# Q's rotary rows computed once per layer for all heads, lists of best tokens sorted by 32, experts' rows on VectorE, and unread products on TensorE ahead of the experts

## The chip, the cores and the metric

The kernel runs on one core of one Trainium2 chip. What counts is the device time of one execution, in microseconds (us); the profile is of one such execution. PE is TensorE, DVE is VectorE, ACT is ScalarE, POOL is GpSimd, SP is SyncE, which here only issues DMA.

## The reference

Two layers over 1024 tokens of 1024 features, batch 1. In each, the normed input goes through one wide projection, three token mixers (attention, pooling, short convolution) are merged by sigmoid gates, one output projection is added back; then each of 16 experts picks the 128 tokens with the highest routing probability for it and works on them.

```python
q = (rmsnorm(cq, q_norm_g) @ w_uq).reshape(B, S, H, DQK)          # 8 heads, 64 + 32 columns
q_rope = apply_rope(q[..., QK_NOPE:], cos[:, :, None], sin[:, :, None])
kv = (rmsnorm(ckv, kv_norm_g) @ w_ukv).reshape(B, S, H, QK_NOPE + V_HEAD)
...
s = jnp.einsum('bqhd,bkhd->bhqk', q_blk, k).astype(jnp.float32)
p = jax.nn.softmax(s, axis=-1).astype(v.dtype)
...
aff = jax.nn.softmax(jnp.einsum('bsd,de->bse', h, w_router), axis=-1)
top_val, top_idx = lax.top_k(aff.transpose(0, 2, 1), cap)          # cap = 128 tokens per expert
xg = jax.vmap(lambda hb, ib: hb[ib])(h, top_idx)
```

## The kernel before

A product of two fp32 matrices is made of three in the type fp32r: each operand is split into a rounded part `hi` (an ACT cast) and the rest `lo` (a DVE subtraction), and `mm3` (L318) issues hi·hi, lo·hi and hi·lo. `split` (L112) is the pair of cast and subtraction. PSUM tiles of 512 columns come from `ps1`, of 1024 from `ps2`.

A layer runs in stages; the times are those of layer 0 in the trace. The projections end around 500 us. The **gate loop** (500 to 622 with the low-rank parts) makes 8 gate blocks, each a projection of 1024 columns on PE and a sigmoid on ACT that is stored to DRAM. The **attention** (622 to 901) goes over 64 units (head h, query block t). For a unit `scores` (L839) makes 12 products of 512 columns into a `ps2` tile, two units ahead; DVE takes the row maximum, ACT the exponential, both share the division; PE transposes the result (`trans`), and every second unit `av` (L868) multiplies with V. K of two heads is made by `k_pair` (L806), Q of one head by `q_head` (L826): 128 output columns, of which 64 are plain and 64 are the rotary ones in two orders, multiplied by a table of cosines and sines (`tab_e`, `tab_o`) and added inside the score product. The weight of a pair is split in seven pieces to get that order. `rope_part` copies the rotated key into K's tiles.

The **merge** (901 to 950) multiplies the attention output by `w_oa`, 16 blocks (half hf, block d) of 12 products each (`merge_mm`, `merge_gate`); two of them run before the last `av`. The **out-projection loop** (950 to 1062, L1235 to L1262) goes over 8 tiles of 128 tokens: two halves of 24 products (`out_mm`), the residual on DVE, four transposes (`x_trans`), and four router products (`router`) per half, the softmax `soft` into `aff`, and the normed row `h2_rows` by ACT and two POOL operations into DRAM. The best tokens of each expert are found alongside on DVE: tiles are collected in `LISTS`, 16 rounds of maxima each, except tiles 6 and 7, which PE transposes so that 4 rounds over 32 columns do (`quick_sort`, `quick_rounds`, `quick_gather`) and then a merging sort (`quick_list`, `quick_merged`). After each residual `fills(FILL)` issues some of this work.

```python
            t = 7
            x_trans(t, 1)
            scale(t)
            router(t, 1)
            quick_gather(6)
            fills(1000)
            ready = soft(t)
            quick_sort(t)
            quick_rounds(t)
            quick_gather(t)
```

What follows (the **tail**, 1062 to 1096) is one chain: the last lists, the least chosen value, masks `mk`, slots `slot_of`, the 0/1 matrix `both` of an expert (L1379), its products with the values `tv` (`chosen`), the indirect load of rows `xg`, their transposes. Then the **experts** run to 1675. Layer 1 does the same up to 3320.

The kernel is written in program order for each engine, with a scheduler's list that puts independent DVE work between steps; `behind(x)` keeps an instruction after x.

Of the kernel before, what the change touches and what calls it, by code (L numbers as in the profile page):

```python
# [42 lines left out]
FILL = 4  # L43
LISTS = ((0, 2), (2, 2), (4, 1), (5, 1))
# [10 lines left out]
def encoder(ctx, tc, x, c, positions, w_mod, b_mod, norm1_g, w_in, b_gate, q_norm_g, w_uq, kv_norm_g,  # L55
# [79 lines left out]
    tabd = dram.tile([2, 128, S], F32, name="tabd")  # L135
# [12 lines left out]
    for q in range(4):  # L148
        for r in range(4):
            DVE.tensor_copy(krsel[32 * r:32 * r + 32, 32 * q:32 * q + 32], ident[0:32, 0:32])  # L150
# [112 lines left out]
    def rope_tables(ip):  # L263
# [29 lines left out]
        one = ip.tile([128, S], F32, name="one", tag="ra")  # L293
        ACT.activation(sn, sn, AF.Copy, scale=sgn)
        DVE.memset(one, 1.0)
        for (i, r, src) in ((0, 0, one), (0, 64, cs), (0, 96, sn), (1, 0, cs), (1, 32, sn), (1, 64, one)):
            n = 64 if src is one else 32
            SP.dma_start(tabd[i, r:r + n, :], src[r:r + n, :])
# [28 lines left out]
    for l in range(DEPTH):  # L327
# [327 lines left out]
        tab_e = Cq.tile([128, S], F32, name="tab_e")  # L655
        SP.dma_start(tab_e, tabd[0])
        tab_o = Cq.tile([128, S], F32, name="tab_o")
        SP.dma_start(tab_o, tabd[1])
        kwhi = Cq.tile([128, 2, 512], F32R, name="kwhi")
        kwlo = Cq.tile([128, 2, 512], F32R, name="kwlo")  # L660
        with pool("cqt", side="left") as cp:
            def low(w, c0):
                p = ps2()
                proj(p, w, c0)
                return p
# [47 lines left out]
            DVE.tensor_mul(kt_[0:64], p[0:64], tab_o[0:64])  # L713
            DVE.tensor_mul(kt_[64:128], p[64:128], tab_e[64:128])
# [12 lines left out]
            split(kwhi, kwlo, raw.rearrange("p k h c -> p k (h c)"))  # L727
            def prepare(pp):
# [24 lines left out]
            for dp in range(4):  # L753
                wg = block()
                for d in (2 * dp, 2 * dp + 1):
# [14 lines left out]
                    POOL.dma_start(gate0d[l][d], g)  # L770
                    if d == 1:
# [6 lines left out]
        with pool("att", side="right") as ap:  # L778
            vt = ap.tile([128, 8, 8, 128], F32R, name="vt")
            khi = [ap.tile([128, S], F32R, name=f"khi{i}") for i in range(4)]  # L780
            klo = [ap.tile([128, S], F32R, name=f"klo{i}") for i in range(4)]
# [24 lines left out]
            def k_pair(hp):  # L806

                raw = ap.tile([128, 3, 192], F32, name="uq", bufs=1)
                SP.dma_start(raw, w_uq[l][:, 192 * hp:192 * hp + 192].rearrange("(k p) f -> p k f", p=128))
                qw[hp] = [ap.tile([128, 3, 256], F32R, name=f"qw{i}", bufs=1) for i in range(2)]  # L810
# [9 lines left out]
                for (d0, s0, n) in ((0, 0, 96), (96, 80, 16), (112, 64, 16),  # L820
                                    (128, 160, 32), (160, 176, 16), (176, 160, 16), (192, 96, 64)):
                    split(qw[hp][0][:, :, d0:d0 + n], qw[hp][1][:, :, d0:d0 + n], raw[:, :, s0:s0 + n])

            def q_head(h):
                w = qw[h // 2]
                i = h % 2  # L826
                cc = slice(128 * i, 128 * i + 128)
                tab = tab_e if i == 0 else tab_o
                qs[h] = W.tile([128, 2, S], F32R, name="raw", tag="raw", bufs=2)
                for q in range(2):  # L830
                    s_ = slice(512 * q, 512 * q + 512)
                    p = ps1()
                    for k in range(3):
                        mm3(p, w[0][:, k, cc], w[1][:, k, cc], cqhi[:, k, s_], cqlo[:, k, s_], k == 0, k == 2)
                    qf = ap.tile([128, 512], F32, name="pexp", tag="pexp", bufs=3)
                    DVE.tensor_mul(qf, p, tab[:, s_])
                    split(qs[h][:, 0, s_], qs[h][:, 1, s_], qf)

            def scores(h, t):  # L839
# [11 lines left out]
                ACT.activation(e, p, AF.Exp, bias=nm, scale=SCALE, accum_out=sm)  # L851
# [52 lines left out]
            last_o = []  # L904
            units = [(h, t) for h in range(H) for t in range(8)]
            es, phl, po = {}, {}, {}
            for t in range(2):
                v_tile(t)
            k_pair(0)
            q_head(0)  # L910
# [4 lines left out]
            for i in range(1, 4):  # L915
                rope_part(i)
            for n, (h, t) in enumerate(units):
                if n + LA < len(units):
# [18 lines left out]
                if h % 2 == 0 and t == 2:  # L937
                    q_head(h + 1)
# [10 lines left out]
                if h % 2 == 1 and h + 1 < H:  # L949
                    if t == 1:  # L950
                        k_pair(h // 2 + 1)
                    if t == 4:
                        q_head(h + 1)
# [13 lines left out]
            pm = [ps2() for _ in range(2)][1]  # L967
            for d in range(2):
                merge_mm(pm[:, 512 * d:512 * d + 512], wo0, 128 * d, 0)
            av(7, 3, *phl.pop((7, 3)), po[7])  # L970
        psum_open(0, 8)
# [34 lines left out]
        split(wo2[0], wo2[1], wo2_raw)  # L1006
        for d in range(2):
            merge_gate(pm[:, 512 * d:512 * d + 512], 0, d)
        for i, (hf, d) in enumerate(merges):
            if i < 2:  # L1010
                continue
            p = ps1()
            wo, c0 = ((wo0, 0), (wo1, 256), (wo2, 512), (wo2, 512))[d // 2]
            merge_mm(p, wo, 128 * d - c0, hf)
# [38 lines left out]
        with pool("wout", side="left") as op_:  # L1053
# [46 lines left out]
            def quick_sort(t):  # L1100

                pt = ps1()
                for g in range(4):
                    PE.matmul(pt[32 * g:32 * g + 32, 0:32], aff[:, t - 1:t + 1, :], (negid if g in (0, 3) else ident)[:, 32 * g:32 * g + 32],
# [459 lines left out]
```

## Time and profile before

| | before |
|---|---|
| time, median of 3 runs | 3343.34 us (3342.88 to 3346.71) |
| the profiled execution: its time, its span | 3343.92 us, 3342.1 us |
| mean granted PE clock | 0.979 |
| PE busy | 3178.8 us (95%) |
| DVE, ACT, POOL busy | 2434.5 (73%), 1857.3 (56%), 346.5 (10%) |
| DMA | 685.90 MB, 205 GB/s over the span |

A granted clock of 1.00 is 2.4 GHz, 0.50 is 1.2 GHz. In a row of instruction groups, `out<-in` are the program's tile names, `[4.92 <-DVE op L884]` is idle time of the engine before the instruction and what ended it.

### The profile page before, as it was taken

How to read it: one execution, taken by the hardware profiler on the slowest of the kernel's cores; microseconds unless marked ns; L12 is line 12 of the kernel's file. 1: busy time of each engine (PE TensorE's matmuls, PEld its weight loads, DVE VectorE, ACT ScalarE, POOL GpSimd, SP SyncE). 2: the span in 40 equal slices, each digit the busy share in tenths (PEclk: the TensorE clock that was granted, in tenths of full speed). 3: DMA queues.
4: the chain of work that ended last, by engine and by line, in shares of the span. 5: the costliest groups of instructions: out<-in, count | busy, mean ns of one | idle time of the engine just before them, and what ended most of it. 6: DMA issues, size and time to landing. Idle time of an engine off the chain costs nothing.

```text
span 3342.1 us, 41527 instructions
## 1 busy us (share of the span) xinstructions
PE 3178.8 (95%) x15825; PEld 2616.3 (78%) x15825; DVE 2434.5 (73%) x3738; ACT 1857.3 (56%) x2535; POOL 346.5 (10%) x356
## 2 busy tenths in 40 slices
PE   6999999999997999999989999999999969999996
PEld 5888887788786788888778888887887858888875
DVE  5555525499868899999854445347998589999997
ACT  5111213488744888887631122226886448888876
POOL 2001011000023001010020000010000331001010
PEclk8999999999998999999999999999999979999998
DMA  6346334100366899999622354340005659999995
GB/s 225 120 138 205 130 125 137 64 18 7 117 221 233 314 394 380 389 389 373 245 60 82 128 165 139 104 164 24 14 28 164 227 211 366 390 390 380 387 381 182
DMA packets 279271, 685.90 MB, mean 205 GB/s; under 512 B 24934, under 2 KB 131648, under 8 KB 279072
## 3 DMA queue, kind: packets, MB, share of 16 engines
q1 hardware_dynamic: 242912, 563.13, 45.5%
q0 software_dynamic: 33856, 111.74, 10.6%
q10 hardware_dynamic: 2304, 8.39, 0.7%
q8 instruction: 124, 2.03, 0.2%
q14 instruction: 75, 0.61, 0.1%
HBM read 607.63 MB, written 75.55 MB: 204 GB/s over the span
## 4 chain that ended last, share of the span: by engine, by line
PE 79%; DVE 12%; ACT 4%; issue 2%; DMA 2%; POOL 1%; SPq 0%; POOLq 0%; DVEq 0%; ACTq 0%
PE ps L325 63%; PE pa L325 4%; PE pa L1149 4%; DVE wlo L115 4%; DVE mx L846 2%; PE pa L864 2%; PE ps L1353 1%; PE pa L872 1%; PE pa L874 1%; ACT whi L115 1%; ACT pexp L851 1%; PE pa L1189 1%; DVE af L1072 1%; DVE pexp L854 1%; DVE T L115 0%
## 5 line engine op out<-in xcount | busy, mean ns | idle before, releaser
L115 DVE TENSOR_TENSOR wlo<-rg,whi 128x1024 fp32r<-128x1024 f32 x768 | 899.6, 1220 | 97.9 <-ACT whi L115 95.1
L115 ACT CAST whi<-rg 128x1024 fp32r<-128x1024 f32 x768 | 763.8, 1048 | 180.1 <-PE ps L325 180.0
L325 PE MATMUL ps<-whi,T 128*128 128x512 f32 x3072 | 841.5, 393 | 3.6 <-ACT T L115 2.2
L325 PEld LDWEIGHTS ps<-whi,T 128*128 128x128 f32 x3072 | 574.4, 189 | 125.6 <-ACT T L115 3.1
L325 PE MATMUL ps<-wlo,T 128*128 128x512 f32 x1536 | 488.1, 399 | 5.0 <-DVE wlo L115 2.6
L325 PE MATMUL ps<-hhi,whi 128*128 128x512 f32 x1376 | 427.3, 392 | 0.0
L325 PE MATMUL ps<-hlo,whi 128*128 128x512 f32 x1376 | 424.0, 389 | 0.0
L325 PE MATMUL ps<-hhi,wlo 128*128 128x512 f32 x1376 | 423.7, 389 | 0.0
L115 ACT CAST whi<-raw 128x2048 fp32r<-128x2048 f32 (+2 forms) x63 | 108.7, 1726 | 428.0 <-PE ps L325 370.5
L325 PEld LDWEIGHTS ps<-wlo,T 128*128 128x128 f32 x1536 | 281.0, 189 | 74.3 <-DVE wlo L115 18.6
L325 PEld LDWEIGHTS ps<-hhi,whi 128*128 128x128 f32 x1376 | 256.9, 188 | 58.8 <-issue 4.2
L325 PEld LDWEIGHTS ps<-hlo,whi 128*128 128x128 f32 x1376 | 258.3, 188 | 54.2
L325 PEld LDWEIGHTS ps<-hhi,wlo 128*128 128x128 f32 x1376 | 258.3, 188 | 54.1
L115 DVE TENSOR_TENSOR wlo<-raw,whi 128x2048 fp32r<-128x2048 f32 (+2 forms) x63 | 130.1, 2065 | 99.9 <-ACT whi L115 99.8
L325 PE MATMUL ps<-khi,raw 128*128 128x512 f32 x512 | 165.8, 405 | 7.2 <-ACT pexp L851 5.7
L115 DVE TENSOR_TENSOR wlo<-pa,whi 128x512 fp32r<-128x512 f32 x256 | 169.5, 681 | 1.1 <-ACT whi L115 0.9
L851 ACT ACTIVATE pexp<-ps,nm 128x1024 f32<-128x1024 f32 x128 | 143.2, 1119 | 30.3 <-DVE nm L848 27.8
L846 DVE TENSOR_REDUCE mx<-ps 128x1 f32<-128x1024 f32 x128 | 155.0, 1213 | 4.3 <-PE ps L325 3.5
L1446 POOL DMA_INDIRECT xres<-y,idx x30 | 72.5, 2416 | 779.4 <-DVE y L1445 779.4
L115 ACT CAST whi<-pa 128x512 fp32r<-128x512 f32 x256 | 139.6, 588 | 6.2 <-PE pa L864 5.0
L229 DVE SCALAR_TENSOR_TENSOR macc<-raw,csil,macc 128x256 f32<-128x256 f32 x280 | 135.0, 484 | 8.4
L864 PE MATMUL pa<-ident,pexp 128*128 128x128 f32 x1024 | 135.2, 273 | 2.6 <-DVE nm L848 1.8
(412 smaller groups left out, 4626.9 us busy)
## 6 DMA issues: line engine op xcount, KB each, us to landing
rg<-in_w_gate_dram SPq DMA_DIRECT2D x128, 1024.0 KB, 8.9
rg<-in_w_up_dram SPq DMA_DIRECT2D x128, 1024.0 KB, 7.0
rg<-in_w_down_dram SPq DMA_DIRECT2D x128, 1024.0 KB, 7.8
raw<-in_w_mod_dram SPq DMA_DIRECT2D x48, 1024.0 KB, 5.3
raw<-in_w_in_dram SPq DMA_DIRECT2D x43, 1024.0 KB, 5.2
part<-pr POOLq DMA_DIRECT2D x32, 512.0 KB, 3.9
pr<-part POOLq DMA_DIRECT2D x16, 512.0 KB, 4.4
sq<-in_w_out_dram POOLq DMA_DIRECT2D x16, 512.0 KB, 4.7
```

Of the source, the lines that this page charges most:

```text
L115: return ACT.copy(hi, src), DVE.tensor_sub(lo, src, f(hi))
L229: DVE.scalar_tensor_tensor(acc, raw[:, k], csil[:, k:k + 1], acc, op0=OP.mult, op1=OP.add)
L325: PE.matmul(dst[:, s], a, b[:, s], start=start and i == 0, stop=stop and i == 2)
L846: DVE.reduce_max(mx, p, axis=AX.X)
L851: ACT.activation(e, p, AF.Exp, bias=nm, scale=SCALE, accum_out=sm)
L854: DVE.tensor_scalar(e[:, :NORM_DVE], e[:, :NORM_DVE], ri, None, op0=OP.mult)
L864: PE.transpose(p[:, 128 * k:128 * k + 128], e[:, o:o + 128], ident)
L872: PE.matmul(po[:, o:o + 256], vt[:, k, h, :], phi[:, k, :], start=(k == 0), stop=False, skip_group_check=True)
L874: PE.matmul(po[0:64, o:o + 256], vt[:, k, h, 0:64], plo[:, k, :], start=False, stop=(k == 7), skip_group_check=True)
L1072: DVE.match_replace(a, v[:, 15 - r, :], a, -1.0)
L1149: PE.matmul(p[c_], a, b, start=(k == 0 and i == 0), stop=(k == 7 and i == 2))
L1446: POOL.indirect_dma_start(out=xres[l], in_=y, in_offset=None, compute_op=OP.add, out_offset=bass.IndirectOffsetOnAxis(ap=idx[e][:, 0:1], a ...
```

## The change

- **Q.** `q_rope` computes the 8 x 32 rotary rows of Q of all heads in one go in gate block 3 (two blocks of 128 rows), rotates them with tables of cosine and sine, splits them and stores them to `qrd` in DRAM. `q_pair` makes the 64 plain columns of two heads at once, and loads the rotary rows of each from `qrd`, held behind the fourth-last exponential. `q_head`, the weight in two orders and the second table go.
- **The attention's start.** K and Q of the first pair come ahead of the V tiles, their weights are loaded in gate block 4, and the rotated key is copied to K's other tiles in units 2, 9 and 17.
- **The merge.** Four blocks instead of two are made before the attention's PSUM tiles are given back, two of them behind the last `av`; the third weight slice is split behind the last sum.
- **The lists.** Tiles 4 to 7 are sorted by 32, `FILL` is 6; `aff_trans` comes one step later. The first half of list 6 is sorted ahead of tile 7's softmax.
- **Rows.** From tile 3 (`OWN`) DVE makes the normed rows in place of ACT and POOL.
- **Unread products.** `keep_on` issues n fp32 products of 128 x 128 into a PSUM tile that nobody reads: 9, 10, 28, 7, 5 and 15 at six places of the tail.
- `both` of expert 0 is made in two halves.

```diff
+    def keep_on(tile_, by, n):
+        with behind(by):
+            for _ in range(n):
+                PE.matmul(tile_, ident, ones, start=True, stop=True, skip_group_check=True)
...
+            def q_rope(raw):
+                w = [W.tile([128, 3, 2, 8, 16], F32R, name=n_, tag=n_) for n_ in ("whi", "wlo")]
...
+                for i in range(2):
+                    p = ps2()
+                    for k in range(3):
+                        mm3(p, w[0][:, k, i], w[1][:, k, i], cqhi[:, k], cqlo[:, k], k == 0, k == 2)
+                    ps.append(p)
...
+                for i, (a, b) in enumerate(((cos, sin), (sin, cos))):
+                    DVE.tensor_mul(r[2 * i], ps[0], a)
+                    DVE.tensor_mul(r[1], ps[1], b)
+                    (DVE.tensor_add if i else DVE.tensor_sub)(r[2 * i], r[2 * i], r[1])
+                    lo = r[2 * i].bitcast(F32R)
+                    split(hi, lo, r[2 * i])
+                    for part, src in enumerate((f(hi), r[2 * i])):
+                        POOL.dma_start(qrd[l][:, 16 * i:16 * i + 16, part, :], src)
...
+            def q_pair(hp):
...
+                    for o in (0, 32):
+                        ld = SP.dma_start(f(qs[h][r + o:r + o + 32]), qrd[l][h])
+                        if last_exp:
+                            gated(ld, last_exp[-4])
...
-                        mm3(p, w[0][:, k, cc], w[1][:, k, cc], cqhi[:, k, s_], cqlo[:, k, s_], k == 0, k == 2)
-                    qf = ap.tile([128, 512], F32, name="pexp", tag="pexp", bufs=3)
-                    DVE.tensor_mul(qf, p, tab[:, s_])
-                    split(qs[h][:, 0, s_], qs[h][:, 1, s_], qf)
+                        mm3(p, w[0][:, k], w[1][:, k], cqhi[:, k, s_], cqlo[:, k, s_], k == 0, k == 2)
+                    for i in range(2):
+                        r = slice(64 * i, 64 * i + 64)
+                        split(qs[2 * hp + i][r, 0, s_], qs[2 * hp + i][r, 1, s_], p[r])
...
             av(7, 3, *phl.pop((7, 3)), po[7])
+            for d in range(2, 4):
+                merge_mm(pms[d], wo1, 128 * d - 256, 0)
...
-        split(wo2[0], wo2[1], wo2_raw)
+        with behind(*last_o[-1]):
+            split(wo2[0], wo2[1], wo2_raw)
...
-                POOL.tensor_mul(xn, xn, a2)
-                POOL.tensor_add(xn, xn, sh2)
+                if t >= OWN:
+                    DVE.scalar_tensor_tensor(xn, xo, rss[t], a2, op0=OP.mult, op1=OP.mult)
+                    DVE.tensor_add(xn, xn, sh2)
...
             def aff_trans(t):
-                if t == 6:
+                if t > 3:
                     quick_sort(t)
                     quick_rounds(t)
                     return
...
-                out_mm(t, p, 1, 4, 7)
-                router(t, 0)
+                out_mm(t, p, 1, 5, 7)
+                if t > 0:
+                    router(t, 0)
+                if t > 4:
+                    quick_gather(t - 1)
                 out_mm(t, p, 1, 7, 8)
...
-            router(t, 1)
-            quick_gather(6)
+            stored = h2_rows(t)
+            idle = ps1()[:, 0:128]
+            keep_on(idle, router(t, 1), 9)
             fills(1000)
+            quick_half(6)
             ready = soft(t)
-            quick_sort(t)
+            keep_on(idle, quick_sort(t), 10)
             quick_rounds(t)
-            quick_gather(t)
+            keep_on(idle, quick_gather(t), 28)
+            with behind(ready):
+                quick_merged(6)
```

On PE, at the end of the loop and in the tail, before (the last out-projection products are L1149, transposes of the residual L1175, gathers of the maxima L1121, router L1189, sort transposes L1104, least value L1298):

```order
2809 L1149 MATMUL pa<-whi,rg 128x512
2810 L1175 MATMUL pa<-ident,xo 128x128 x4
2811 L1121 MATMUL pa<-topl,negid 16x32
2812 L1121 MATMUL pa<-topl,ident 16x32
...
2815 L1189 MATMUL pa<-wra,hT 128x16 x4
2816 L1104 MATMUL pa<-negid,aff 32x32
2817 L1104 MATMUL pa<-ident,aff 32x32 x2
2818 L1104 MATMUL pa<-negid,aff 32x32
...
2822 L1121 MATMUL pa<-topl,ident 16x32
2823 L1298 MATMUL pa<-ident,least 128x16
```

and now (L1216, L1246, L1181, L1260, L1163, L1389 in the same roles):

```order
2762 L1216 MATMUL pa<-whi,rg 128x512
2763 L1181 MATMUL pa<-topl,negid 16x32
2764 L1181 MATMUL pa<-topl,ident 16x32
...
2767 L1246 MATMUL pa<-ident,xo 128x128 x4
2768 L1260 MATMUL pa<-wra,hT 128x16 x4
2769 L130 MATMUL pa<-ones,ident 128x128 x9
2770 L1163 MATMUL pa<-negid,aff 32x32
...
2772 L1163 MATMUL pa<-negid,aff 32x32
2773 L130 MATMUL pa<-ones,ident 128x128 x10
...
2777 L1181 MATMUL pa<-topl,ident 16x32
2778 L130 MATMUL pa<-ones,ident 128x128 x28
2779 L1389 MATMUL pa<-ident,least 128x16
```

The gather of tile 6 moved from behind the residual's transposes to ahead of the last residual, and the unread products (L130) stand between the steps of the chain.

On DVE, at the merge, before (`gh` is a merge gate, `op` the sum of the last head pair, `olo` its rest, `wlo<-raw` of 2048 columns the third weight slice):

```order
750 L986 TENSOR_TENSOR gh<-ps,gh 128x512 x2
751 L987 TENSOR_TENSOR gh<-gh 128x512 x2
752 L115 TENSOR_TENSOR wlo<-raw,whi 128x2048
753 L884 TENSOR_TENSOR op<-pa,otmp 64x512
754 L115 TENSOR_TENSOR olo<-op,ohi 128x512
755 L115 TENSOR_TENSOR rg<-gh,rg 128x512 x2
```

and now:

```order
707 L1045 TENSOR_TENSOR gh<-ps,gh 128x512 x2
708 L1046 TENSOR_TENSOR gh<-gh 128x512 x2
709 L941 TENSOR_TENSOR op<-pa,otmp 64x512
710 L117 TENSOR_TENSOR olo<-op,ohi 128x512
711 L117 TENSOR_TENSOR wlo<-raw,whi 128x2048
712 L117 TENSOR_TENSOR rg<-gh,rg 128x512 x2
```

The sum and its split now stand ahead of the weight slice.

## Rows read from the trace of the kernel before

**Rows 1.** Windows: us, busy us per engine (instructions), PE clock, DMA share, GB/s.

```profile
560.00:620.00 60.00, 60.00 (x268) 49.69 (x267) 13.39 (x15) 8.35 (x7) 10.13 (x19) 1.00 0.52 174
620.00:640.00 20.00, 16.56 (x71) 12.77 (x70) 12.35 (x21) 11.27 (x21) 0.53 (x1) 1.00 0.17 57
640.00:660.00 20.00, 18.17 (x100) 15.23 (x99) 16.86 (x34) 16.40 (x28) 0.00 (x0) 1.00 0.00 0
670.00:860.00 190.00, 188.63 (x1195) 164.56 (x1194) 176.72 (x353) 159.62 (x292) 1.60 (x3) 1.00 0.06 21
904.00:910.30 6.30, 4.03 (x10) 3.16 (x11) 4.17 (x5) 1.66 (x3) 0.00 (x0) 0.50 0.57 206
1020.00:1060.00 40.00, 37.67 (x202) 30.87 (x201) 38.28 (x176) 20.10 (x38) 16.55 (x10) 1.00 0.42 160
1064.40:1068.00 3.60, 2.11 (x16) 1.99 (x16) 1.29 (x9) 2.72 (x5) 0.00 (x0) 0.50 1.01 413
```

**Rows 2.** PE's waits, 900 to 1062: line, releaser, us in total, times, longest.

```profile
PE pa L325 <- DVE op L884: 4.9, 1, 4.9
PE pa L1221 <- DVE aff L1201: 2.4, 3, 0.8
...
PE pa L1104 <- DVE aff L1201: 0.8, 1, 0.8
```

**Rows 3.** Timeline of PE, tail: start us, us, instruction, [idle before <-releaser].

```profile
1064.46 1.89 PE L1189 MATMUL pa<-wra,hT 128*128 128x16 f32 x8 [0.40 <-DVE hT L1178]
...
1074.68 0.29 PE L1121 MATMUL pa<-topl,negid 128*16 128x32 f32 x2 [6.57 <-DVE topl L1113]
...
1084.06 0.25 PE L1298 MATMUL pa<-ident,least 16*128 16x16 f32 x1 [8.77 <-DVE least L1296]
...
1094.65 1.97 PE L1364 MATMUL pa<-ident,xg 128*128 128x128 f32 x8 [4.00 <-DMA xg<-h2d,idx]
1096.44 1.22 PE L325 MATMUL ps<-whi,T 128*128 128x512 f32 x2
...
1098.30 1.09 PE L325 MATMUL ps<-whi,T 128*128 128x512 f32 x4
```

**Rows 4.** Timeline of PE at the merge.

```profile
906.27 0.80 PE L325 MATMUL pa<-ohi,whi 128*128 128x512 f32 x1 [4.92 <-DVE op L884]
...
909.85 0.63 PE L325 MATMUL pa<-ohi,wlo 128*128 128x512 f32 x1
...
911.34 0.39 PE L325 MATMUL pa<-olo,whi 128*128 128x512 f32 x1
...
913.85 0.39 PE L325 MATMUL pa<-ohi,whi 128*128 128x512 f32 x1
```

**Rows 5.** Instruction groups, 620 to 902: count, busy us, mean ns, idle before.

```profile
L325 PE MATMUL pa<-cqhi,qw 128*128 128x512 f32 x96 | 31.1, 392 | 1.4 <-ACT qw L115 1.4
...
L115 DVE TENSOR_TENSOR klo<-pa,khi 64x512 fp32r<-64x512 f32 x16 | 10.6, 683 | 1.8 <-ACT khi L115 1.7
```

**Rows 6.** DMA issues, 620 to 900: count, KB each, median us to landing.

```profile
gh<-gate SPq DMA_DIRECT2D x3, 256.0 KB, 3.2
```

**Rows 7.** Timeline of ACT and of DVE at the merge.

```profile
901.28 1.90 ACT L115 CAST whi<-raw 128x2048 fp32r<-128x2048 f32 x1 [4.36 <-PE pa L872]
...
903.21 2.29 DVE L115 TENSOR_TENSOR wlo<-raw,whi 128x2048 fp32r<-128x2048 f32 x1 [1.19 <-ACT whi L115]
```

**Rows 8.** Timeline of DVE and of POOL in the tail.

```profile
1068.29 0.20 DVE L1089 TENSOR_TENSOR ll<-ll 16x64 f32<-16x64 f32 x1
...
1068.53 2.27 DVE L1090 TENSOR_TENSOR ll<-ll 16x64 f32<-16x64 f32 x1
...
1071.28 2.27 DVE L1090 TENSOR_TENSOR ll<-ll 16x64 f32<-16x64 f32 x1
...
1068.38 2.34 POOL L1211 TENSOR_TENSOR xn<-xn,a 128x1024 f32<-128x1024 f32 x1 [4.64 <-ACT xn L1210]
```

**Rows 9.** Timeline of PE in the low-rank part (fp32 products L685).

```profile
510.23 1.88 PE L685 MATMUL ps<-sq,ones 128*128 128x512 f32 x4
...
512.41 0.63 PE L325 MATMUL ps<-hlo,whi 128*128 128x512 f32 x2
```

More of the change, by code (lines that the diff above doesn't have):

```diff
@@ L134, in encoder @@
     gate0d = [dram.tile([8, 128, S], F32, name=f"gate0{l}") for l in range(DEPTH)]
-    tabd = dram.tile([2, 128, S], F32, name="tabd")
+    tabd = dram.tile([3, 128, S], F32, name="tabd")
+    qrd = [dram.tile([8, 32, 2, S], F32, name=f"qrd{l}") for l in range(DEPTH)]
     woutd = [dram.tile([8, 128, D], F32, name=f"woutd{l}") for l in range(DEPTH)]
@@ L147, in encoder @@
     krsel = consts.tile([128, 128], F32, name="krsel")
-    for q in range(4):
+    DVE.memset(krsel, 0.0)
+    for q in (0, 2):
         for r in range(4):
@@ L292, in rope_tables @@
         DVE.tensor_scalar(sgn, sgn, 0.125, -1.0, op0=OP.mult, op1=OP.add)
[L293 to L298, printed above, removed]
+        turned = ip.tile([128, S], F32, name="turned", tag="ra")
+        ACT.activation(turned, sn, AF.Copy, scale=sgn)
+        SP.dma_start(tabd[0], cs)
+        SP.dma_start(tabd[1], sn)
+        for (r, src) in ((0, cs), (32, turned), (64, cs), (96, turned)):
+            SP.dma_start(tabd[2, r:r + 32, :], src[r:r + 32, :])
     def rms_scale(src, n, scr):
@@ L806, in k_pair @@
             def k_pair(hp):
-                raw = ap.tile([128, 3, 192], F32, name="uq", bufs=1)
-                SP.dma_start(raw, w_uq[l][:, 192 * hp:192 * hp + 192].rearrange("(k p) f -> p k f", p=128))
-                qw[hp] = [ap.tile([128, 3, 256], F32R, name=f"qw{i}", bufs=1) for i in range(2)]
+                raw = uq0 if hp == 0 else uq_load(hp)
+                qw[hp] = [ap.tile([128, 3, 2, 64], F32R, name=f"qw{i}", bufs=1) for i in range(2)]
+                split(qw[hp][0], qw[hp][1], raw.rearrange("p k (i c) -> p k i c", c=96)[:, :, :, 0:64])
                 cc = slice(128 * hp, 128 * hp + 128)
@@ L914, in encoder @@
                 v_tile(t)
-            for i in range(1, 4):
-                rope_part(i)
             for n, (h, t) in enumerate(units):
+                if n in (2, 9, 17):
+                    with behind(last_exp[-1]):
+                        rope_part((2, 9, 17).index(n) + 1)
                 if n + LA < len(units):
@@ L1154, in residual @@
                 added = DVE.tensor_add(xo[:, s_], xo[:, s_], p[hf])
+                if t == 7:
+                    if hf == 0:
+                        gained[t] = op_.tile([128, D], F32, name="xn", tag="xo", bufs=3)
+                    DVE.tensor_mul(gained[t][:, s_], xo[:, s_], a2[:, s_])
                 scr = op_.tile([128, 512], F32, name="hT", tag="hT", bufs=3)
@@ L1207, in h2_rows @@
                 POOL.dma_start(xres[l][sl, :], xo)
-                xn = op_.tile([128, D], F32, name="xn", tag="xo" if t == 7 else "xn", bufs=3 if t == 7 else 1)
-                with behind(softs[-1]):
-                    ACT.activation(xn, xo, AF.Copy, scale=rss.pop(t))
-                POOL.tensor_mul(xn, xn, a2)
-                POOL.tensor_add(xn, xn, sh2)
+                if t == 7:
+                    xn = gained.pop(t)
+                    DVE.scalar_tensor_tensor(xn, xn, rss[t], sh2, op0=OP.mult, op1=OP.add)
+                    return POOL.dma_start(h2d[l][sl, :], xn)
+                xn = op_.tile([128, D], F32, name="xn", bufs=1)
+                if t >= OWN:
+                    DVE.scalar_tensor_tensor(xn, xo, rss[t], a2, op0=OP.mult, op1=OP.mult)
+                    DVE.tensor_add(xn, xn, sh2)
+                else:
+                    with behind(softs[-1]):
+                        ACT.activation(xn, xo, AF.Copy, scale=rss[t])
+                    POOL.tensor_mul(xn, xn, a2)
+                    POOL.tensor_add(xn, xn, sh2)
                 return POOL.dma_start(h2d[l][sl, :], xn)
             def aff_trans(t):
-                if t == 6:
+                if t > 3:
                     quick_sort(t)
@@ L1242, in encoder @@
                 out_mm(t, p, 0, 0, 3)
+                if t == 1:
+                    router(0, 0)
                 if t > 0:
@@ L1286, in encoder @@
             prefetch(PF[0])
-            stored = h2_rows(t)
-            with behind(ready):
-                quick_merged(6)
             last = l == DEPTH - 1
@@ L1377, in choose @@
                     away = hot[e] = ep.tile([128, 8, 128], BF16, name="both")
+                    if e == 0:
+                        for hf in range(2):
+                            h_ = slice(4 * hf, 4 * hf + 4)
+                            DVE.tensor_tensor(hot[e][:, h_], slots_far[:, None, :].to_broadcast([128, 4, 128]),
+                                              slot_of[:, h_, e:e + 1].to_broadcast([128, 4, 128]), op=OP.is_equal)
+                        return
                     if e < 2:
@@ L1423, in encoder @@
             prefetch(PF[1], stored)
+            idle = ps2()[:, 0:128]
             choose(0)
```

125 lines of the change are left out of this document (79 added, 46 removed).

## The prediction

> **What bounds the kernel now.** I read the windows first, by stage: a stage in which TensorE (PE) is busy for nearly all of the stretch gets shorter only by products that go away. In the gate loop PE is busy for 60.00 of 60 us. In the middle of the attention it is busy for 188.63 of 190 us, with DVE at 176.72 close behind [rows 1]. So a product added to the first costs its full time and one taken from the second saves it. The exceptions are four places where PE stands still, which I looked up in PE's waits and in the timeline. At the attention's start PE is busy for 16.56 and 18.17 of 20 us [rows 1]. At the merge it waits 4.9 us for the last head pair's sum [rows 2], and then runs at the granted clock of 0.50, the lower level of 1.2 GHz, until 910.3 [rows 1]. In the out-projection loop it waits 2.4 us for the softmax's `aff` [rows 2]. In the tail, from the last router product at 1064.46 to the first expert product at 1096.44, that is 32.0 us, PE mostly waits for a serial chain on DVE [rows 3], and the clock is at 0.50 [rows 1]. Layer 1 repeats all of this: the sums below are for one layer, and count twice.
>
> **A, rotating Q in the gate loop: +8.5.** Two blocks of 128 output rows, 3 slices of depth, 3 products, 2 halves: 36 products of 512 columns. Back to back one takes 0.228 us (from 911.34 to 913.85 are 11 of them [rows 4]). 36 x 0.228 = 8.2, on a PE that has no gap there. The weight split and six DVE passes over a row block lie beside it: DVE is busy for 13.39 of 60 us, ACT for 8.35 [rows 1]. I add 0.3 for the first product's wait for its split; 0 to 2 are the bounds. Four stores of 512 KB go onto POOL's queue, three loads with short rows and three of tables onto SP's; with the DMA engines busy at 0.52 [rows 1] and four more gate products ahead of their first reader, they cost nothing.
>
> **B, products per head in the attention: -16.3.** Today a head costs 18 products of its own: a layer has 96 with cqhi [rows 5], two of each three, and half as many with cqlo. Then a pair of heads costs 18: 72 fewer, 72 x 0.228 = 16.4, taken as 16.3. This is worth its time only if DVE gives way too, as it is busy for 93% of the stretch. It does: a pass over 512 columns takes 0.68 us [rows 5], also on half the rows. A layer loses 16 multiplications and 16 subtractions of that width and gains 16 subtractions: 16 x 0.68 = 11 us less. One split of the weights per pair in place of seven takes off some 4 more, an estimate. That is nearly PE's saving. The rotated rows must be loaded: four loads of 256 KB per pair on SP's queue, held until the fourth-last exponential is done. A load of that size lands after 3.2 us [rows 6], and from the place where they are issued (unit 4 of the odd head) to the first scores that read them are two units, 8.7 us (64 units take some 280 us). Behind them on SP stand only merge operands needed much later. No wait is counted.
>
> **C, the attention's start: -4.3.** PE loses 3.44 and 1.83 us in the two windows [rows 1], 5.3 in all. The edit loads the weights earlier, makes one split of seven, and moves three copies of K's rotated half to later units, where ACT (159.62 of 190 us busy) takes them. The first products still need a free PSUM tile and that split; I leave 1 us. Bounds: 0 and -5.3.
>
> **D, the merge: -6.0.** Behind the last product, at 901.35 (906.27 less 4.92 [rows 4]), ACT first casts the third weight slice (1.90 us) and DVE subtracts it (2.29 us), and only then the sum is made [rows 7]; PE goes on at 906.27. Then 9 products run at half clock, 0.45 us each (from 906.27 to 909.85 are 8 [rows 4]), 9 x (0.45 - 0.23) = 2.0 more. Together 6.9. Now 24 products, 5.5 us at full clock, stand right behind the last one, and the slice is split behind the sum. The chain to the split's end is then a copy, an addition, a cast, 1.90 and 2.29, about 6.1 us: the third of the next products, at 5.9, waits up to 0.5. Bounds: -3 (if the chain is 3 us longer) and -6.9.
>
> **E, the loop: -1.5.** `aff` waits fall, since DVE no longer shares the time with POOL's row arithmetic: a DVE step of 0.20 takes 2.27 beside a POOL operation of 2.34 [rows 8]. At most the 3.2 us of both `aff` rows are regained [rows 2]. Against it: DVE, busy for 38.28 of the last 40 us [rows 1], gets those rows itself, two passes of a 1024-wide row for tiles 3 to 6, some 2.5 us a tile by the 0.68 of a 512-wide one; the sort by 32 repays most of this. And PE now waits for it in a new place: the gather of tiles 4 to 6 stands ahead of the last three products, while DVE still has up to 24 instructions (for tile 6) from `aff` to the last maximum. At 0.20, somewhat overlapped, that is some 3.5 us, against 1.8 us of PE's work, six products and a half router. Behind that gather wait three products and the residual. I take half of the 3.2 as gained. Bounds: -4 and +5.
>
> **F, the tail: -6.0.** Two DVE steps of 2.27 that POOL's rows slowed become steps of 0.20: -4.1 [rows 8]. The first half of list 6 is sorted while PE and ACT do the softmax, 14 of 53 steps leave the last stretch: at 0.20 it would be 2.8, they overlap, so -1.6. If the clock is held at its upper level by the unread products, 8 transposes from 1094.65 to 1096.44 and four products from there to 1098.30 [rows 3] take half: 0.9 + 0.9 = -1.8. Against it: tile 7's row goes onto DVE ahead of the softmax, and the first nine unread products stand ahead of the sort's transposes. An fp32 call of 512 columns takes 0.86 us: from 510.23 to 512.41 are two of them and two products [rows 9], (2.18 - 0.46) / 2. A quarter of it, 0.215, is one unread product at full clock, an estimate. Nine take 1.9 us at full and 3.9 at half clock, and at 1064.4 the clock is low [rows 1]: +1.5. The other groups (10, 28, 7, 5, 15) then take 2.2, 6.0, 1.5, 1.1 and 3.2 us, inside waits of about 2.4, 6.5, 1.8, 1.5 and 4.0 (today's 6.57 and 8.77 [rows 3] and 4.00, less what DVE saves). Nothing is counted for them. Bounds: -9 and +9.
>
> **Sum.** 8.5 - 16.3 - 4.3 - 6.0 - 1.5 - 6.0 = -25.6 for a layer, -51.2 for both. The profiled execution took 3343.92 us (its span of 3342.1 and 1.8 around it), 0.6 above the median of 3343.34; so 3343.3 - 51.2 = 3292 us.
>
> **Rivals.**
> - *The clock is not held.* The unread products then run at half clock, and overrun their waits by about 1.2, 1.9, 5.5, 1.3, 0.6 and 2.5, 13 us in all; the 1.8 are lost too. 14.8 x 2: 3322 us. For it: fp32 work in the tail, transposes and router products, did not bring the clock back before 1098.3 [rows 1, 3]. Against it: that work was short with long gaps, and the fp32 calls at 510.23 [rows 9] lie in a stretch without a gap in PE's work. By the Trainium skill (TensorE: Matmul & The Clock Gate, Part 4) a transpose does not count as PE-busy in the same way. If products against an identity in fp32 were treated likewise, this rival would hold. They are plain products, though, and after the eight transposes of rows 3 the clock came back 1.9 us behind the first expert product, while at the merge it took 4.0 from the first product: here transposes seem to have counted.
> - *The attention does not follow PE.* If the chain of exponentials or DVE sets its pace, B is worth nothing: +16.3 x 2, 3325 us. For it: DVE at 93%. Against: PE at 99% with hardly a wait, and DVE loses nearly as much work.
> - *DVE falls behind in the loop.* E at +5 instead of -1.5: 13 us, 3305 us. For it: 38.28 of 40; against: in those 40 us are DVE steps that POOL had slowed.
> - *Slower: rotated rows come late.* If the loads for pairs 1 to 3 are stuck on SP's queue behind the gate on the exponentials or a buffer, PE waits at each pair's first scores. Six such waits eat the gain from 51.2 / 6 = 8.5 us each on, which needs a landing 17 us after issue in place of 3.2; at 10 us each the time is 3352. For it: the queue is in order. Against: DMA is busy at 0.06 there [rows 1], and three buffers serve two heads.
> - The change may also miss its merge (D at -3): 3298, inside the range.
>
> **Numbers.** Forecast 0.62; DVE behind 0.13; clock 0.11; attention 0.07; late rows 0.04; the rest unnamed. Low end: with C, D, E and F near their good bounds (-5.3, -6.9, -4, -9) a layer gives -33; 3277, and some room below it for what I counted at nothing: 3270. The high end takes in the first two rivals: 3325. A measurement here tells 0.2%, 6.7 us, from no change. Faster by more than that: 0.91, being all cases but late rows and some of a mix of rivals; within it 0.04; slower 0.05.
>
> **What would show it.** A: 36 more products in the gate loop, no new idle time. B: 96 and 48 products become 48 and 24, the attention ends about 12 us earlier after its start, PE still dense. D: PE's wait for the sum below 1 us and the clock at 1.00 through the merge. E: waits for the gathered maxima below 2 us in all. F: no DVE sort step over 0.4 us, the clock back at 1.00 by some 1070, first expert product 26 us behind the last router product. Wrong would be: half clock through the tail, PE waiting for loaded rows of Q, or an attention that keeps its length.

## The result, and the profile after

The changed kernel takes 3304.84 us (median of 4 runs, 3303.79 to 3307.26) against 3343.55 before: a ratio of 0.9883, 95% interval 0.9866 to 0.9901, or 38.7 us less. Forecast were 51 us less; the time lies inside the range of 3270 to 3325. The page of the profiled execution:

```profile
span 3302.5 us, 42120 instructions
...
PE 3196.3 (97%) x16109; PEld 2630.6 (80%) x16109; DVE 2416.1 (73%) x3652; ACT 1844.8 (56%) x2489; POOL 303.2 (9%) x344
```

PE is busier although 39.6 us of span went, because the products that nobody reads count as busy. Where the time went is read from the first and last starts of a few lines. Layer 0 before, by source line (count, ns min/median/max, first to last start):

```profile
L872 PE MATMUL pa<-whi,vt x256: 276/278/386, 655.2 to 901.0; 128*128 128x256 f32 x128
L1149 PE MATMUL pa<-rg x192: 387/392/486, 946.5 to 1053.2; 128*128 128x512 f32 x192
L1149 PE MATMUL pa<-whi,rg x128: 388/395/500, 951.9 to 1061.3; 128*128 128x512 f32 x128
L1364 PE MATMUL pa<-ident,xg x8: 418/418/474, 1094.6 to 1096.2; 128*128 128x128 f32 x8
```

and after:

```profile
L929 PE MATMUL pa<-whi,vt x256: 274/278/387, 658.0 to 890.5; 128*128 128x256 f32 x128
L1216 PE MATMUL pa<-rg x192: 387/392/797, 929.5 to 1045.4; 128*128 128x512 f32 x192
L1216 PE MATMUL pa<-whi,rg x128: 388/395/628, 935.0 to 1052.7; 128*128 128x512 f32 x128
L1456 PE MATMUL pa<-ident,xg x8: 273/273/328, 1079.5 to 1080.3; 128*128 128x128 f32 x8
```

The attention's start is the first product of its own: before, that of a V tile, behind a wait of 1.25 us; now, that of K, with no wait.

```profile
622.98 0.50 PE L325 MATMUL pa<-whi,ckhi 128*128 128x512 f32 x1 [1.25 <-ACT cf L769]
```

```profile
629.17 0.39 PE L336 MATMUL pa<-ckhi,kwhi 128*128 128x512 f32 x1
```

The stages are:

| us | before, layer 0 / 1 | after | difference | forecast term |
|---|---|---|---|---|
| start of the attention (layer 0) | 623.0 | 629.2 | +6.2 | A +8.5, less 1.3 of C |
| attention | 278.0 / 278.3 | 261.3 / 259.9 | -16.7 / -18.4 | B -16.3, rest of C -3.0 |
| merge, to the loop's first product | 45.5 / 45.8 | 39.0 / 39.1 | -6.5 / -6.7 | D -6.0 |
| out-projection loop | 114.8 / 115.2 | 123.2 / 121.1 | +8.4 / +5.9 | E -1.5 |
| tail, to the row transposes | 33.3 / 33.2 | 26.8 / 26.7 | -6.5 / -6.5 | F -6.0, with the next line |
| experts of 0 and projections of 1; last experts | 1176.0; 599.0 | 1178.3; 597.9 | +2.3; -1.1 | A of layer 1 +7.2, and clock |

One stage went the wrong way: the loop. Loop and tail together took 148.1 and 148.4 us before and take 150.0 and 147.8 now, so what the tail gained the loop lost. The loop's length also varies between profiles of the same code: in five of them (the change, and four runs below that leave the loop alone) it lies between 119.9 and 123.2 us, which is 4.8 to 8.4 more than before. The timeline of PE there shows why it is longer:

```profile
996.01 0.66 PE L1246 MATMUL pa<-ident,xo 128*128 128x128 f32 x4 [2.56 <-DVE xo L1221]
...
1016.45 0.40 PE L1216 MATMUL pa<-whi,rg 128*128 128x512 f32 x1
1018.11 0.23 PE L1181 MATMUL pa<-topl,negid 128*16 128x32 f32 x2 [1.27 <-DVE topl L1173]
...
1018.45 2.35 PE L1216 MATMUL pa<-rg 128*128 128x512 f32 x9
...
1035.57 0.27 PE L1181 MATMUL pa<-topl,negid 128*16 128x32 f32 x2 [2.77 <-DVE topl L1173]
...
1036.09 4.21 PE L1216 MATMUL pa<-rg 128*128 128x512 f32 x9
```

PE waits for a residual of tile 3, and for the maxima of tiles 4 and 5. The gather stands ahead of the tile's last three products in the source, but behind them in the trace (the last at 1016.45, the gather at 1018.11): what it holds up are the first nine products of the next tile. Behind the last wait nine products take 4.21 us, where behind the shorter one before they took 2.35: the clock has fallen. The windows say the same (columns as in [rows 1]). Before the change the clock was at 1.00 over the whole loop; this is its middle:

```profile
930.00:1050.00 120.00, 116.06 (x590) 96.12 (x589) 80.99 (x271) 55.36 (x97) 37.04 (x27) 1.00 0.56 204
```

and now:

```profile
930.00:1050.00 120.00, 112.74 (x591) 92.28 (x590) 76.31 (x292) 49.65 (x96) 22.76 (x22) 0.96 0.54 204
980.00:1000.00 20.00, 17.27 (x82) 13.61 (x81) 12.86 (x43) 6.29 (x13) 5.11 (x5) 0.93 0.90 342
1000.00:1020.00 20.00, 18.73 (x110) 15.29 (x109) 17.63 (x67) 8.36 (x17) 1.59 (x3) 0.98 0.26 101
1020.00:1040.00 20.00, 17.23 (x92) 13.98 (x91) 17.59 (x89) 6.63 (x15) 1.34 (x3) 0.87 0.14 58
```

The first wait is no lack of DVE time: DVE is busy for 12.86 of the 20 us from 980 on. DVE's timeline:

```profile
988.93 0.21 DVE L1149 TENSOR_TENSOR best<-best 16x64 f32<-16x64 f32 x1
992.26 1.28 DVE L1286 SCALAR_TENSOR_TENSOR xn<-xo,rs,a 128x1024 f32<-128x1024 f32 x1 [3.12 <-DMA h2d<-xn]
```

Tile 3's row, the first that DVE makes, wants the single buffer `xn`, from which tile 2's row, made by ACT and POOL, is still being stored. The residual is queued behind it.

### The profile page after: what moved, and what is told of

Same layout as the page of the kernel before. It is cut to its first block, busy times and chain, and to the rows that moved or that the text cites. A ratio compares the mean times of both kernels' runs of the same rounds, so it can differ in the third digit from the quotient of the medians.

```text
span 3302.5 us, 42120 instructions
## 1 busy us (share of the span) xinstructions
PE 3196.3 (97%) x16109; PEld 2630.6 (80%) x16109; DVE 2416.1 (73%) x3652; ACT 1844.8 (56%) x2489; POOL 303.2 (9%) x344
## 5 line engine op out<-in xcount | busy, mean ns | idle before, releaser
L117 ACT CAST whi<-raw 128x2048 fp32r<-128x2048 f32 (+3 forms) x67 | 110.6, 1654 | 430.3 <-PE ps L336 373.7
L117 DVE TENSOR_TENSOR wlo<-raw,whi 128x2048 fp32r<-128x2048 f32 (+3 forms) x67 | 132.1, 1975 | 97.2 <-ACT whi L117 97.2
L921 PEld LDWEIGHTS pa<-ident,pexp 128*128 128x128 f32 x1024 | 116.9, 140 | 27.1 <-PE ps L336 9.8
```

Source lines behind the costliest of these rows:

```text
L117: return ACT.copy(hi, src), DVE.tensor_sub(lo, src, f(hi))
L921: PE.transpose(p[:, 128 * k:128 * k + 128], e[:, o:o + 128], ident)
```

## The experiments

**The loop.** *Rows from tile 0 on DVE:*

```diff
-OWN = 3
+OWN = 0
```

> All normed rows are made by DVE (tiles 0 to 6 instead of 3 to 6), so no row waits for the store of one that POOL made. Theory 1 (the out-projection loop got longer because DVE stands for 3.1 us before tile 3's row, until tile 2's row has left its only buffer, and PE then waits 2.6 us for the residual): this wait goes in both layers, with the half clock behind it, and 3 to 4 us a layer come back: about 3298. Theory 2 (DVE simply has too much work in the loop): three more rows of 2.5 us on DVE make it 3 to 7 us a layer slower: 3312 or more.

3299.32 us, ratio 0.9868 (0.9852 to 0.9885). The loop took 117.6 and 115.4 us, 5.6 and 5.7 less, though DVE makes three more rows; the tail gave 2.7 and 1.5 of it back. Theory 2 is out: DVE does more and the loop gets shorter. DVE's wait for the buffer is gone, and the clock stays at 1.00 from 980 to 1040. That fits theory 1, but the edit also takes the rows of tiles 0 to 2 off POOL, and one `aff` step that took 1.3 us in the change takes 0.2 again; so some 1 us of the gain can be that.

*The gathers later:*

```diff
+                if t > 5:
+                    quick_gather(t - 2)
+                    fill.append(lambda t=t: quick_merged(t - 2))
...
-                if t > 4:
-                    quick_gather(t - 1)
...
             x_trans(t, 1)
+            quick_gather(6)
```

> The gathers of tiles 4, 5 and 6 on PE are put where other products or an idle time cover DVE's rounds: tiles 4 and 5 into the next tile, behind its first nine products, tile 6 behind the last transposes. Theory 1 (PE waits 1.3 and 2.8 us for the rounds because the gather stands in the middle of its products, and runs at half clock for some us behind the second wait): both waits and the half clock at 1036 go, 4.0 us and 2 to 4 us of clock a layer: about 3292. Theory 2 (DVE's backlog is the bound, and PE waits for the residual instead): the waits move to the residual and the time stays within 3 us of 3305.

3304.43 us, ratio 0.9879 (0.9861 to 0.9897). Neither theory as stated: the loop did get shorter, to 116.6 and 115.2 us, but the tail grew from 27 to 31 us. The waits for the maxima were real: they fell from 4.0 to 1.2 us. The time is what theory 2 said, but not by its way: the waits for the residual grew by 0.8 us at most, and the tail took the rest. Why the tail grew is not shown here; that tile 6's list comes later is the obvious guess, and the run after the next speaks against it.

*Both:*

> Both edits together. If the two waits are separate causes, the gains add: 3.5 and 6.5 us a layer, about 3285, and the loop takes 114 us a layer, as before the change. If DVE's total work is the bound, less than half of that is left: 3296 or more.

3295.59 us, ratio 0.9854 (0.9837 to 0.9870). Loop 113.0 and 113.2 us, shorter than before the change; tail 30.3 and 30.0. In the loop most of the two gains adds up: 10.2 and 7.9 us of 12.2 and 11.6. The tail takes back 3.5 and 3.3. For the whole kernel 9.3 us are left of the 20 that adding would have given, so the time is the one that the second theory gave (3296), and 10 us from the first (3285).

*Tile 6's gather left where the change has it:*

```diff
-                if t > 4:
+                if t == 7:
                     quick_gather(t - 1)
```

(with the moves of tiles 4 and 5 and rows from tile 0 as above)

> Rows from tile 0 on DVE and the gathers of tiles 4 and 5 in the next tile, with tile 6's gather left ahead of the last three products, where the change has it. With all three gathers moved the loop took 113 us, but the tail 30 instead of 27: PE's clock had fallen before the first unread products, and tile 6's list came late. Theory 1 (it is tile 6's gather that lengthens the tail): the loop stays at 113 to 115 us, the tail comes back to 27 to 28: 3289 to 3293. Theory 2 (what is saved in the loop only makes DVE late in the tail): the tail stays at 30 and the time at 3295 to 3298.

3304.66 us, 0.9888 (0.9870 to 0.9906): a miss. The loop stays at 113.7 and 112.7, but the tail takes 34.8 and 33.6. PE waits 4.3 us for the maxima at tile 6's gather. The gather stands behind the loop's last product, so the wait counts in the tail, which is 4.5 and 3.6 us longer than with both edits. Theory 1 is out: it was not the later gather of tile 6 that lengthened the tail. That the last list's work is a fixed amount on DVE, which holds up PE wherever the gather is put, fits the four runs but is argued. What is measured is that loop and tail trade: together they take 150.0 and 147.8 us in the change, 147.1 and 143.6 with rows from 0, 147.6 and 146.4 with later gathers, 143.3 and 143.2 with both, 148.5 and 146.3 here.

*The clock held through the waits:*

```diff
+                if 4 < t < 7:
+                    keep_on(ps1()[:, 0:128], m, (5, 12)[t - 5])
```

> The change with 5 and 12 more unread products ahead of the gathers of tiles 4 and 5 in the loop, about as long as PE waits there (1.1 and 2.6 us at full clock). The waits themselves stay. Theory 1 (half of what the loop lost is the half clock behind those waits): the clock stays at 1.00 between 1020 and 1055, 2 to 4 us a layer come back: 3297 to 3301. Theory 2 (the waits alone are the loss): 3303 to 3307.

3302.30 us, 0.9873 (0.9855 to 0.9890). The clock stayed at 1.00 from 930 to 1050:

```profile
930.00:1050.00 120.00, 115.61 (x651) 95.50 (x649) 79.61 (x313) 50.93 (x100) 22.79 (x22) 1.00 0.57 211
```

The loop took 119.0 and 118.8 us, where five profiles with the same loop (the change, and the runs with one unread product at each place, with either old merge and with 448 columns, below; both layers) lie between 119.9 and 123.2. Only a part of what theory 1 gave to the clock came back, some 1 to 4 us a layer, and 1.2 and 1.4 of that went in the tail (28.0 and 28.1). The median lies between the two theories, and its interval overlaps the change's.

*Rows back to POOL:*

```diff
-OWN = 3
+OWN = 7
```

> Tiles 3 to 6 have their normed rows made by ACT and POOL, as before the change; only tile 7's is DVE's. Theory 1 (POOL's row work stretches DVE's small steps from 0.2 to 2.3 us beside it, so that DVE is better off with the rows itself): DVE steps of 2 us are back in the loop, PE waits longer for the maxima and the loop gets 2 to 6 us a layer longer: 3309 to 3317. Theory 2 (the rows on DVE, 2.5 us each, and the wait for the row buffer cost more than they save): the 2.6 us wait at tile 3 goes and the loop gets shorter: 3295 to 3302.

3330.20 us, 0.9958 (0.9943 to 0.9972), worse than either theory said: loop 130.7 and 129.5 us, tail 31. The DVE timeline has the stretched steps back, here one of four of 2.2 to 2.4 us in the layer's loop:

```profile
1049.22 2.41 DVE L1148 TENSOR_TENSOR best<-best 16x64 f32<-16x64 f32 x1
```

and PE's timeline the waits behind them:

```profile
1032.64 0.23 PE L1163 MATMUL pa<-negid,aff 128*32 128x32 f32 x1 [2.84 <-DVE aff L1273]
...
1054.96 0.19 PE L1163 MATMUL pa<-negid,aff 128*32 128x32 f32 x1 [3.35 <-DVE best L1149]
```

With the sorting by 32 in the loop, rows on DVE are worth 25.4 us. The amount of stretching does not explain that by itself: these four steps and two `aff` steps of 1.3 us take some 11 us a layer more than the same steps elsewhere, about as much as the 10 us of row work that DVE is rid of. They lie in the chain that PE waits for, as the two waits show; that this is all of the rest is not shown.

**The merge.** *As before the change:*

```diff
-            for d in range(2, 4):
-                merge_mm(pms[d], wo1, 128 * d - 256, 0)
...
-        with behind(*last_o[-1]):
-            split(wo2[0], wo2[1], wo2_raw)
+        split(wo2[0], wo2[1], wo2_raw)
...
-            if i < 4:
+            if i < 2:
```

> The merge as before the change: two blocks ahead of the last attention product, and the third weight slice split ahead of the last sum. Theory 1 (the reordering took 6.5 us a layer out of the merge, as the stage lengths 45.5 and 39.0 say): the merge takes 45 to 46 us again, PE waits 4.9 us for the sum, the clock is at 0.50 for some us: 3317 to 3319. Theory 2 (the gain there is only moved, and later stages take it up): less than 3 us a layer, 3310 or less.

3306.94 us, 0.9892 (0.9874 to 0.9910), and a merge of 38.4 us, shorter than the change's own 39.0. Both theories fail: what I had counted as the cause is taken out, and the gain stays. (One thing is not as before: the two early blocks lie in the first `ps2` tile, where they lay in the second.) PE goes straight on:

```profile
890.56 0.28 PE L931 MATMUL pa<-wlo,vt 128*64 128x256 f32 x1
890.68 0.40 PE L336 MATMUL pa<-ohi,whi 128*128 128x512 f32 x1
```

while DVE still splits the weight first and then makes the sum, as in [rows 7]:

```profile
892.70 2.29 DVE L117 TENSOR_TENSOR wlo<-raw,whi 128x2048 fp32r<-128x2048 f32 x1 [1.20 <-ACT whi L117]
895.03 0.69 DVE L941 TENSOR_TENSOR op<-pa,otmp 64x512 f32<-64x512 f32 x1
```

The first block doesn't need this sum (it works on the other half of the tokens). What it needed before was a PSUM bank: in the program before, the last attention product's result and the first block behind it both have bank 0, and the sum is the last to read it. In the change and in this run that result lies in bank 1. *The same bank again,* by three unread products in tiles of their own ahead of the old merge, which leave bank 1 to the first block:

```diff
+        for _ in range(3):
+            PE.matmul(ps1()[:, 0:128], ident, ones, start=True, stop=True, skip_group_check=True)
```

> The merge as before the change, which alone kept PE free of a wait, with three short unread products in PSUM tiles of their own ahead of the first merge block. They do no more than turn the choice of banks on: the first block then gets the bank that holds the last attention product's result, as it did before the change. Theory 1 (the wait at the merge was one for that bank, whose last reader is the sum on DVE; the change removed it by shifting the banks, not by the two added blocks and the later split): PE waits 4 to 5 us for the sum again, at half clock behind it, the merge takes 44 to 46 us instead of 38.4, and the time is 3317 to 3321. Theory 2 (the first products had to wait for the sum for another reason, that is gone in any case): 3306 to 3309, the three products alone.

3320.30 us, 0.9931 (0.9915 to 0.9948); merge 46.4 and 46.3 us. PE's waits from 885 to 932 are the one of [rows 2] again, for the same instruction:

```profile
PE pa L336 <- DVE op L941: 4.2, 1, 4.2
```

and its timeline has the three products (six records) at once, and the wait behind them:

```profile
890.89 0.83 PE L1065 MATMUL pa<-ones,ident 128*128 128x128 f32 x6
895.97 0.80 PE L336 MATMUL pa<-ohi,whi 128*128 128x512 f32 x1 [4.25 <-DVE op L941]
```

Against the run before, these three products and the banks behind them are all that differs, and the wait is back: theory 1 is shown. Why the result moved to bank 1 is argued: `q_pair` asks for two PSUM tiles a pair where `q_head` asked for two a head, and no run has that alone. Nor was the change's own order run with the shared bank, so whether the two named edits would have hidden the wait by themselves is open.

**The tail.** *One unread product at each place:*

```diff
-            for _ in range(n):
+            for _ in range(min(n, 1)):
```

> One unread product instead of 9, 10, 28, 7, 5 and 15 at each of the six places. Theory 1 (they hold the clock in the tail and cost little time themselves): the clock falls to 0.50 soon after 1056, the row transposes take 1.8 us again instead of 0.9, the first four expert products 1.9 instead of 0.9, small PE steps a few tenths: 2 to 3 us a layer slower, 3309 to 3311. Theory 2 (they overrun their gaps by more than the clock gives): a little faster, 3301 to 3304.

3308.74 us, 0.9894 (0.9877 to 0.9910), 3.9 us slower than the change. With the unread products the tail's steps are dense on PE (two records are one product):

```profile
1056.27 2.25 PE L130 MATMUL pa<-ones,ident 128*128 128x128 f32 x18
...
1062.13 6.52 PE L130 MATMUL pa<-ones,ident 128*128 128x128 f32 x56
1069.77 0.20 PE L1389 MATMUL pa<-ident,least 16*128 16x16 f32 x1 [1.12 <-DVE least L1387]
...
1079.51 1.09 PE L1456 MATMUL pa<-ident,xg 128*128 128x128 f32 x8 [0.27 <-DMA xg<-h2d,idx]
1080.84 0.73 PE L336 MATMUL ps<-whi,T 128*128 128x512 f32 x2 [0.24 <-ACT T L117]
```

Without them the windows show the clock at 0.50 from 1056 on, and the transposes take their 1.97 us of [rows 3] again:

```profile
1060.00:1066.00 6.00, 0.23 (x2) 0.00 (x0) 5.72 (x39) 0.00 (x0) 0.00 (x0) 0.50 0.92 326
```

```profile
1077.07 1.97 PE L1456 MATMUL pa<-ident,xg 128*128 128x128 f32 x8 [3.07 <-DMA xg<-h2d,idx]
1078.86 1.22 PE L336 MATMUL ps<-whi,T 128*128 128x512 f32 x2
```

The tail to the transposes is only 0.7 and 0.9 us longer (27.5 and 27.6); from the transposes' start to the eleventh expert product it is 5.9 us (1077.07 to 1082.96) instead of 3.7 (1079.51 to 1083.24). So some 3 us a layer are the clock's, and of the tail's gain 5.8 us stay without it (33.3 before, 27.5 here). The median shows less than these 3 us twice, as the loop, which the edit leaves alone, is 2.5 and 1.0 us shorter in this profile.

The run also answers a reading of the prediction, that the eight transposes seem to have helped to bring the clock back. Before the change the four products at 1098.30, 1.9 us behind the first expert product, were at full clock [rows 3]. Here, behind the same eight transposes, they still take 1.91 us:

```profile
1080.73 1.91 PE L336 MATMUL ps<-whi,T 128*128 128x512 f32 x4
1082.44 0.69 PE L336 MATMUL ps<-wlo,T 128*128 128x512 f32 x2
1082.96 1.09 PE L336 MATMUL ps<-whi,T 128*128 128x512 f32 x4
```

The clock is back only by 1082.96, 4.1 us behind the first. Whether transposes count is open.

*More of them, around tile 7's transposes:*

```diff
+            keep_on(idle, last_mm, 3)
+            keep_on(idle, x_trans(t, 1), 5)
```

(with rows from 0, later gathers and the old merge)

> Rows from tile 0 on DVE, all three gathers later, the merge as before, and 3 + 5 more unread products around tile 7's last transposes, where PE's clock fell when both loop edits were made (3295.6). If the clock then stays up at the start of the tail, its first nine unread products take 1.9 us instead of 4.2 and the tail 27 to 28 us instead of 30; the merge gives 0.6: 2.5 to 3.5 us a layer, 3289 to 3291. If DVE's work sets the tail, 3293 to 3296.

3297.78 us, 0.9860 (0.9843 to 0.9876): no gain. The clock is held at first (1.00 from 1040 to 1052), but the tail takes 31.2 in both layers, as PE then only waits longer for DVE:

```profile
1051.62 0.22 PE L1160 MATMUL pa<-negid,aff 128*32 128x32 f32 x1 [2.80 <-DVE aff L1272]
```

**The attention.** *Less of the division on DVE:*

```diff
-NORM_DVE = 512
+NORM_DVE = 448
```

> The change with 448 instead of 512 of the 1024 columns of the softmax's division on DVE, the rest on ACT. Theory 1 (the attention got 1.5 to 3 us a layer less shorter than 72 products are worth because DVE, busy for 94%, now sets the pace): 64 units, some 0.05 us less each on DVE, and the attention gets 1 to 3 us a layer shorter: 3299 to 3303. Theory 2 (ACT, busy for 89%, is as close to the bound, or PE's own spacing is the rest): no difference of more than 1 us a layer, 3304 to 3308.

The attention took 259.2 and 258.7 us, 2.1 and 1.2 less, as theory 1 had it, and less than in every profile with 512 columns (259.6 at least). Yet the median was 3304.90 us, ratio 0.9881 (0.9865 to 0.9898), no different from the change. In the profile the layer 1 experts are 2.3 us longer than the change's, which the edit doesn't touch; so the stage's gain is shown, that of the whole isn't.

**The best.** *Rows from 0, later gathers, old merge, 448:*

> Rows from tile 0 on DVE, all three gathers later, the merge as before the change (its first block in a free bank) and 448 columns of the division on DVE. If the gains of the separate edits add, 3295.6 less 1.2 (merge, 0.6 a layer) less 3.3 (attention, 2.1 and 1.2): 3291. If the attention's gain is lost again, as it was in the median of the run that had it alone: 3294 to 3296.

3293.61 us (median of 5 runs), 0.9849 (0.9835 to 0.9862): between the two cases. It is 51 us faster than before and 11 faster than the change. Against both loop edits alone (3295.59, 0.9837 to 0.9870) the 2 us are inside the noise.

## Why the prediction was right, and where it failed

The time came inside a range that was 55 us wide. B's mechanism was right and its size nearly; D's size was right by luck; E failed, and alone it missed by 17.3 us in the two layers, more than the 12.5 by which the whole missed.

**A, +8.5.** About 7.5: 6.2 later, and 1.3 of the start's wait gone. PE has no new wait there; 36 products at 0.228 are 8.2, and the 0.7 between is not traced.

**B and C, -16.3 and -4.3.** Together -18.0 and -19.7 of 20.6 (with the 1.3). The start gave all that was counted: from the end of the gate loop at 621.7 to the first product with V were 33.5 us, now from 629.2 to 658.0 28.8. In the steady part 13.3 and 14.8 came of 16.3: DVE was a little closer to the bound than I took it to be. It is busy for 94% of the time now (150.26 of 160 us), and PE no longer for all of it:

```profile
700.00:860.00 160.00, 156.30 (x1010) 136.43 (x1009) 150.26 (x290) 142.30 (x253) 1.59 (x3) 1.00 0.16 47
```

The run with 448 columns got 2.1 and 1.2 of the missing 3.0 and 1.5 back; the rest is open. The loads of rotated rows, the rival on the slower side, landed after 4.1 and 4.3 us, and no wait of PE names them:

```profile
raw<-qrd SPq DMA_DIRECT2D x8, 256.0 KB, 4.1
q<-qrd SPq DMA_DIRECT2D x4, 256.0 KB, 4.3
```

**D, -6.0.** The size was right (6.5 and 6.7), the cause not the one I named, so that this is luck. I read "the wait for the sum" as a need of the data and priced the reordered split and the added blocks; it was a wait for a bank, and it went as Q's new code, most likely by asking for fewer tiles, left the result in another. With the two named edits taken out, the gain stayed; with the bank shared again, it went. The two edits were not needed here; whether they would have been enough with the shared bank, no run shows.

**E, -1.5.** This is the step that failed: +8.4 and +5.9, outside its bounds of -4 to +5 (in the four other profiles with this loop +4.8 to +8.1). The sign that I had set, waits for the gathered maxima below 2 us in all, came out at 4.0. I named PE's wait at the gathers and its size (up to 1.7 us a tile; 1.3 and 2.8 came), but had it hold up the last three products and the residual, where in the trace it held up the next tile's. I set it against a gain in `aff`, and left out two things. One is the single row buffer at the first tile that changes hands from POOL to DVE, 3.1 us of DVE. The other is what a wait in the middle of the products costs behind it, at half clock (4.21 us for nine products in place of 2.35), of which I had just priced the same at the merge. Rival "DVE falls behind in the loop" was the right one in kind, at 13 us; the loop lost more than that against the forecast, 9.9 and 7.4. That the measured time is nearly this rival's 3305 is chance, as other terms came out better. Its reason was only in part DVE's load: more rows on DVE made the loop shorter.

**F, -6.0.** -6.5 to the transposes, and 1.3 and 1.4 more to the eleventh expert product. No step of the lists on DVE takes over 0.4 us in the tail now, where two took 2.27 [rows 8]: 4.1 us, two thirds, as counted. How the rest of the 5.8 that stay without the clock divides, no run shows. The clock gave some 3 against the run with one product at each place, where I had 1.8 less 1.5. The nine first unread products ran at full clock, 2.25 us, not half, as the clock had not yet fallen at 1056. The rival that the clock isn't held is out: plain fp32 products against an identity did hold it, at 1.00 from 1050 to 1084, where with one at each place it was at 0.50 from 1056 to 1078. So in this case, by the runs, what the Trainium skill says of transposes (TensorE: Matmul & The Clock Gate, Part 4) doesn't carry over to such products.

## What to carry to other kernels

When PE "waits for DVE", ask what for: the value, or the place that the other engine is the last to read. Here the wait for a place went when the result had another bank, and came back when three more tiles were asked for.

Where a job passes from one engine to another in the middle of a loop, look at the buffer at the seam. Move a consumer in PE's queue only to where its producer is surely done, read its place from the trace and not from the source, and price a stall inside a dense stretch with the half clock that can follow it (behind the 2.77 us wait here, not behind the 1.27). Judge two neighbouring stages by their sum: here what the tail gained the loop lost.

## What was not expected

Three products a layer that nobody reads, 0.8 us of work, made the kernel 13 us slower (3306.94 to 3320.30), by moving the first merge block to another bank in each layer. And a DVE step of 0.2 us beside a POOL operation takes 2.2 to 2.4 in the loop, as it took 2.27 in the tail [rows 8]: giving four rows a layer back to POOL cost 25 us (3330.20 against 3304.84), 12.7 a layer, where DVE spends only some 10 us a layer on them.
